# A hybrid recurrent and convolution block: other spacing of the heads' chains, 16x16 blocks copied on GpSimd, weight adds and one transpose placed by hand

## The chip, the cores and the metric

The kernel runs on one core of one Trainium2 chip. It is one launch with all inputs and the output in the chip's memory. The metric is the device time of one execution in microseconds (us). Engines are named as in the profile: PE is the matrix engine (PEld its weight loads), DVE the vector engine, ACT the scalar engine, POOL is GpSimd, and SP issues most of the loads and stores. Each engine works through its own instructions strictly in the order in which they were built into its queue; semaphores hold an instruction until its inputs are there and its output's buffer is free, and whatever stands behind it in the queue waits too.

## The reference

One layer for 512 tokens of width 1024, all in float32: a gated delta rule with 8 heads of 128, beside it a convolution branch, both gated and summed, then a SwiGLU feed-forward of width 2816 and a last norm.

```python
h = rmsnorm(x, norm1_w)
q, k, v, z, b_raw, a_raw, glu, gates = split(h @ w_in)
q, k, v = silu(causal_conv4(q, k, v));  q, k = l2norm(q), l2norm(k)
o = gated_delta_rule_chunked(q, k, v, g, beta)        # 8 heads
out_a = (rmsnorm(o, dn_norm_w) * silu(z)) @ dn_w_o
c = causal_conv31(ga * sigmoid(gb))
out_b = silu(layernorm(c)) @ cm_w_pw2 + cm_b_pw2
x = x + (gate_a * out_a + gate_b * out_b) @ w_out
h2 = rmsnorm(x, norm2_w)
x = x + (silu(f_gate) * f_up) @ ffn_w_down            # f_gate, f_up = split(h2 @ w_gate_up)
return rmsnorm(x, norm_f_w)
```

## The kernel before

Every large matmul is made as three passes of a shorter format. A weight block of 128x1024 is loaded as `raw`, ACT rounds it to `whi` (L107), DVE subtracts to get the rest, `wlo` (L108), and `split3` issues the passes (hh,whi), (hl,whi), (hh,wlo) at L117, where `hh` and `hl` are the rounded value and the rest of the activations. There are three buffers for such weight units. Outputs are tiles of 128 channels by 512 tokens, so most matmuls are 512 wide.

The program has these parts, with their times in the profile of before:

- 0 to about 85 us: input norm, transposes, the small projections, the first convolution inputs.
- about 85 to 350: the eight heads. `head` (L713) makes four projections of a head (k, q, v, z); `front` (L397) and `front2` (L451) make the head's small matrices for its four chunks of 128 tokens, and `chain` (L467) the four steps of the recurrence (L540 to L573). The heads' projections are interleaved with "other" projections (the convolution branch's `glu`, then gates), handed out by `take(8)`.
- to 483: the rest of the gates; then to about 533 the output projection `wo` of the heads (L812), among it the layer norm of the convolution branch: `ln_mean` (L629) at tile 2, `ln_norm` (L645) at tile 5.
- to 580 `wpw`, to 623 `wout` with the second norm and its transposes (L883 to L905), to 859 the feed-forward's first half, to 973 the down projection (`two`, L1119) and the last norm.

A `step` is about an eighth of a projection (three matmuls 512 wide); `count` numbers the steps. A chain for head n is begun once `count` has come to `START + ROUND * n` (84 + 40 n), and each of its pieces then says after how many steps the next one comes. Its pieces are put `behind()` the marked instructions of the large stream, which pins their place on each engine. Every 40 steps `background()` issues pieces of the 31-tap convolution (`conv31`, L612, 30 operations of DVE for each of eight channel blocks).

In `front` the inverse of a triangular 128x128 matrix is begun with 16x16 blocks: `Un` (L419 ACT, L420 POOL) is the matrix; four copies `cp` take its 32x32 diagonal blocks (L425, ACT), `cc` picks the two 16x16 blocks of each (L427 ACT, L428 DVE), `cc` is stored and loaded again in another layout as `U` (L430, L433, SP), and GpSimd solves the blocks in 30 small operations (L446, L448). `Ud` (L437, POOL) is the masked `Un`. `front2` makes `Vp` (L456, ACT, four pieces), read from a matmul result `g` of which there are two buffers; in the recurrence `w` (L552, ACT) takes a result of PE from `st`, and PE's next matmul of the chain (L555) needs `w`.

GpSimd also adds weights ahead of time. Sums of the down projection's blocks are made in halves: a load (`U`, later `wsh`, one buffer), four adds (`dsums_add`, L167) and a store (`wsum`, L168). The other stream is `s` (L191): DMAs with an add, issued from GpSimd's queue. In the layer norm, GpSimd sums the squares in seven adds (L642, tile `sacc`), and PE's matmul at L647 reads that sum.

At the end of `wout`, PE transposes the third block of tokens (`transposes(2)`), starts the first three tiles of the feed-forward on the first 256 tokens (`k_loop` over `first`, 256 wide), then transposes the fourth block (`transposes(3)`); ACT and DVE make `hh` (L904) and `hl` (L905) of each.

Of the kernel before, what the change touches and what calls it, by code (L numbers as in the profile page):

```python
# [6 lines left out]
F32 = mybir.dt.float32  # L7
# [16 lines left out]
PAD3 = 368  # L24
START = 84
ROUND = 40
EPS = 1e-6


@with_exitstack  # L30
def block_kernel(ctx, tc, a):
# [131 lines left out]

    def dsums_add(k, r, cs=slice(0, T)):
        b11, b12, b21, b22 = (r[:, i, :] for i in range(4))
        for o, x, y in ((b22, b12, b22), (b12, b11, b12), (b11, b22, b11), (b21, b11, b21)):
            G.tensor_tensor(out=o, in0=x, in1=y, op=ALU.add)  # L167
        nc.gpsimd.dma_start(wsum[k][:, :, cs], r)  # L168

    def half_load():  # L170
# [214 lines left out]

    def decay(h):

        DT = gp.tile([P, NT, P], F32, name="DT", bufs=2)
        nc.sync.dma_start(DT.rearrange("p n t -> p (n t)"),
                          mrow[h].rearrange("n t -> (n t)").partition_broadcast(P))  # L390
        G.tensor_tensor(out=DT, in0=DT, in1=neg.rearrange("p (a t) -> p a t", a=1).broadcast_to([P, NT, P]),
                        op=ALU.add)
        for n in range(NT):
            S.activation(DT[:, n, :], DT[:, n, :], AF.Exp, bias=nmc[:, n, h:h + 1])
        return DT

    def front(h, kT, DT):  # L397
        sq = junk[:, 0:P]

        ss = gp.tile([P, 8, NT], F32, name="ss", bufs=5)  # L400
        ps = tok(kT, psg, "g")
        for n in range(NT):
            S.activation(sq, ps[:, n, :], AF.Square, accum_out=ss[:, 0, n:n + 1])
        kd = gp.tile([P, 3, P], F32, name="kd", bufs=3)
        for n in range(3):
            S.activation(kd[:, n, :], ps[:, n, :], AF.Copy, scale=kdf[:, n, h:h + 1])
        kk, rk, nk, nb2, b2 = ss[:, 3], ss[:, 4], ss[:, 5], ss[:, 6], ss[:, 7]
        V.tensor_scalar(out=kk, in0=ss[:, 0], scalar1=EPS, scalar2=None, op0=ALU.add)
        V.reciprocal(out=rk, in_=kk)
        G.tensor_tensor(out=nk, in0=kk, in1=root4, op=ALU.pow)  # L410
        V.tensor_tensor(out=nb2, in0=rk, in1=nbeta[:, :, h], op=ALU.mult)
        V.tensor_tensor(out=b2, in0=rk, in1=beta[:, :, h], op=ALU.mult)

        ps = psg.tile([P, 4, P], F32, name="g")
        for n in range(NT):
            PE.matmul(ps[:, n, :], kT[:, n, :], kT[:, n, :], start=True, stop=True)
        Un = gp.tile([P, NT, P], F32, name="Un", bufs=3)
        for n in range(NT):
            S.activation(Un[:, n, :], ps[:, n, :], AF.Copy, scale=nb2[:, n:n + 1])  # L419
        G.tensor_tensor(out=Un, in0=Un, in1=DT, op=ALU.mult)  # L420

        cp = gp.tile([P, NT, 32], F32, name="cp")
        for b in range(4):
            b32 = slice(32 * b, 32 * b + 32)
            S.copy(out=cp[b32], in_=Un[b32, :, b32])  # L425
        cc = gp.tile([P, NT, 16], F32, name="cc")
        S.activation(cc, cp[:, :, 0:16], AF.Copy, scale=mh1)  # L427
        V.scalar_tensor_tensor(out=cc, in0=cp[:, :, 16:32], scalar=mh2, in1=cc, op0=ALU.mult, op1=ALU.add)  # L428
        sc = dram.tile([8, 16, NT, 16], F32, name="sc")
        nc.sync.dma_start(sc.rearrange("b k n c -> (b k) n c"), cc)  # L430
        U = gp.tile([P, 16, NT, 16], F32, name="U", bufs=2)
        for b in range(8):
            nc.sync.dma_start(U[16 * b:16 * b + 16].rearrange("p k n c -> p (k n c)"),  # L433
                              sc[b].rearrange("k n c -> (k n c)").partition_broadcast(16))

        Ud = gp.tile([P, NT, P], F32, name="Ud", bufs=3)
        G.tensor_tensor(out=Ud, in0=Un, in1=mc.rearrange("p (a t) -> p a t", a=1).broadcast_to([P, NT, P]),  # L437
                        op=ALU.mult)


        y = gp.tile([P, NT, 16], F32, name="y", bufs=3)
        S.copy(out=y, in_=idc.rearrange("p (a c) -> p a c", a=1).broadcast_to([P, NT, 16]))
        for k in range(15):
            w = 15 - k
            tm = gp.tile([P, NT, 16], F32, name="ytm")
            G.tensor_tensor(out=tm[:, :, 0:w], in0=U[:, k, :, k + 1:],  # L446
                            in1=y[:, :, k:k + 1].broadcast_to([P, NT, w]), op=ALU.mult)
            last[0] = G.tensor_tensor(out=y[:, :, k + 1:], in0=y[:, :, k + 1:], in1=tm[:, :, 0:w], op=ALU.add)  # L448
        return ss, kd, b2, Un, Ud, y
# [207 lines left out]
    def step():  # L657

        while queue:
            try:  # L660
                next(queue[0])
            except StopIteration:
                queue.pop(0)
                continue
            count[0] += 1
            if count[0] % ROUND == 0:
                background()
            return True
        return False
# [85 lines left out]
    rest = others()  # L755
    for h in range(H):
        queue.append(head(h, done))
        queue.append(take(8))
    queue.append(rest)
    nh = 0  # L760
    while step() or chains:
        start_feed[0] = count[0] >= 335
        if nh < H and count[0] >= START + ROUND * nh:
            chains.append([0, chain(*done[nh])])
            nh += 1
        for c in list(chains):
            if c[0] <= count[0] or not queue:
                with behind():
                    n = next(c[1], None)
                if n is None:  # L770
                    chains.remove(c)
                else:
                    c[0] = count[0] + n
# [104 lines left out]
    def norm2(hf, n, cs):  # L878
        rms_half(ss2, hf, n, cs, tp.tile([P, T], F32, name="sg"), hf)
        if hf:  # L880
# [4 lines left out]
            if n == NT - 1:  # L885

                transposes(2)
                for f in (0, FF, 1):
                    first.append((psw.tile([P, T], F32, name="w"), unit(a["wgu"][f])))
                for ps, w in first:  # L890
                    k_loop(ps, w, slice(0, 2 * P))
                transposes(3)

    def transposes(n):

        ts = slice(n * P, (n + 1) * P)
        for j in range(2):
            ps = psm.tile([P, 4, P], F32, name="mm")
            with behind(mybir.EngineType.PE):
                for c in range(4):  # L900
                    k = 4 * j + c
                    PE.transpose(ps[:, c, :], xs2[:, n, k * P:(k + 1) * P], ident)
            k4 = slice(4 * j, 4 * j + 4)
            S.activation(hh[:, k4, ts], ps, AF.Copy)  # L904
            V.tensor_tensor(out=hl[:, k4, ts], in0=ps, in1=hh[:, k4, ts].bitcast(F32), op=ALU.subtract)  # L905

    first = []

# [210 lines left out]
    def two(weights, xs, banks, then, also=(), k0=0):  # L1119
# [3 lines left out]
        for k in range(FK):  # L1123
# [3 lines left out]
                    nc.sync.dma_start(*also.pop(0))  # L1127
            for i in range(2):
                prods(w, i, xs[k], i, banks[2 * i:2 * i + 2], k == 0, k == FK - 1)
            if left:  # L1130
                with behind():
                    left.pop(0)()
            if k > 1:
# [153 lines left out]
```

## Time and profile before

| | |
|---|---|
| median of three runs | 975.8 us (973.53 to 977.41) |
| the profiled execution | 975.02 us |
| its span, first to last instruction | 973.2 us |
| PE busy | 942.7 us, 97% |
| DVE busy | 730.4 us, 75% |
| ACT busy | 537.9 us, 55% |
| POOL busy | 347.9 us, 36% |
| granted clock of PE, mean | 0.995 of full speed |

PE is the engine to follow: it is busy for nearly the whole span, so the time can only fall where PE stands still or is slow, and only grows where PE is made to wait. In a timeline row the first number is the start, the second the length; in brackets stands how long the engine was idle before and which instruction ended that. A matmul 512 wide has a length of some 0.39 us but the next one starts 0.227 us after it, since they are pipelined; distances between starts are what counts.

### The profile page before, as it was taken

To read this page: it belongs to the slowest core of one execution; us is meant where nothing else is said; L and a number is where in the kernel's file an instruction comes from. 1 tells how busy PE (TensorE), PEld (TensorE's weight loads), DVE (VectorE), ACT (ScalarE), POOL (GpSimd) and SP (SyncE) were. 2 spreads that over 40 slices of the span, in tenths; PEclk is the share of its full clock that TensorE was granted. 3 is DMA by queue.
4 is the path that set the end of the run, shared out by engine and by line. 5 is a ranking of instruction groups with operands and counts; after the bars stand their busy time and mean duration, and the time that the engine had idled before them with its cause. 6 is when DMAs were issued, how large, how long until landed. Compare 5 with 4: busy or idle time off the path is not lost. (4 is left out here: it accounts for less than half of the span.)

```text
span 973.2 us, 14887 instructions
## 1 busy us (share of the span) xinstructions
PE 942.7 (97%) x5199; PEld 795.3 (82%) x5199; DVE 730.4 (75%) x1125; ACT 537.9 (55%) x1130; POOL 347.9 (36%) x516
## 2 busy tenths in 40 slices
PE   7999999999999999999998999999999999999996
PEld 5687878878787888888886888888889999988875
DVE  4898988878888868889667753666434787789775
ACT  6688768678767573543536332333323554556544
POOL 0314524424252345254253442254441111134225
PEclk9999999999999999999999999999999999999998
DMA  8233422313222247688987985488899656577654
GB/s 316 86 128 100 142 78 66 99 44 122 81 84 89 76 132 217 180 258 286 299 253 233 272 254 162 174 242 281 282 266 222 205 174 196 171 225 246 225 180 143
DMA packets 78300, 177.40 MB, mean 182 GB/s; under 512 B 10209, under 2 KB 19329, under 8 KB 77201
## 3 DMA queue, kind: packets, MB, share of 16 engines
q1 hardware_dynamic: 66816, 144.88, 44.7%
q0 software_dynamic: 10256, 28.89, 12.9%
q10 hardware_dynamic: 1152, 2.69, 0.7%
q8 instruction: 41, 0.67, 0.3%
q14 instruction: 35, 0.28, 0.1%
HBM read 156.22 MB, written 45.37 MB: 207 GB/s over the span
## 5 line engine op out<-in xcount | busy, mean ns | idle before, releaser
L107 ACT ACTIVATE whi<-raw 128x1024 fp32r<-128x1024 f32 (+1 forms) x191 | 196.2, 1029 | 253.4 <-PE mm L117 154.3
L108 DVE TENSOR_TENSOR wlo<-raw,whi 128x1024 fp32r<-128x1024 f32 (+1 forms) x191 | 239.6, 1255 | 93.8 <-ACT whi L107 92.7
L117 PE MATMUL mm<-hh,whi 128*128 128x512 f32 (+1 forms) x688 | 269.5, 392 | 0.0
L117 PE MATMUL mm<-hl,whi 128*128 128x512 f32 (+1 forms) x688 | 263.5, 383 | 2.3 <-POOL hl L298 1.7
L117 PE MATMUL mm<-hh,wlo 128*128 128x512 f32 (+1 forms) x688 | 264.7, 385 | 0.5 <-DVE wlo L108 0.5
L612 DVE SCALAR_TENSOR_TENSOR cps<-c,c31w,cps 128x512 f32<-128x512 f32 x240 | 180.0, 750 | 5.7 <-ACT cps L610 1.6
L117 PEld LDWEIGHTS mm<-hl,whi 128*128 128x128 f32 x688 | 129.9, 189 | 24.7 <-POOL hl L298 2.9
L117 PEld LDWEIGHTS mm<-hh,wlo 128*128 128x128 f32 x688 | 129.6, 188 | 24.3 <-DVE wlo L108 0.9
L117 PEld LDWEIGHTS mm<-hh,whi 128*128 128x128 f32 x688 | 129.8, 189 | 21.0 <-ACT hh L297 0.2
L939 POOL TENSOR_TENSOR fm<-fm 128x256 f32<-128x256 f32 x33 | 30.1, 914 | 113.7 <-DVE s L939 91.9
L446 POOL TENSOR_TENSOR ytm<-U,y 128x60 f32<-128x60 f32 (+14 forms) x120 | 37.4, 311 | 53.3 <-DMA U<-sc 39.0
L370 DVE SCALAR_TENSOR_TENSOR acc<-mm,c4w,acc 128x511 f32<-128x511 f32 (+2 forms) x72 | 53.0, 738 | 2.1 <-ACT acc L367 1.7
L117 PE MATMUL mm<-yh,whi 128*128 128x512 f32 x128 | 51.3, 401 | 0.0
L117 PE MATMUL mm<-yh,wlo 128*128 128x512 f32 x128 | 50.5, 395 | 0.0
L117 PE MATMUL mm<-yl,whi 128*128 128x512 f32 x128 | 50.3, 393 | 0.0
L117 PE MATMUL w<-hl,whi 128*128 128x256 f32 x168 | 47.5, 283 | 1.1 <-DVE hl L905 1.1
L117 PE MATMUL w<-hh,wlo 128*128 128x256 f32 x168 | 47.6, 284 | 0.8 <-DVE wlo L108 0.8
L117 PE MATMUL w<-hh,whi 128*128 128x256 f32 x168 | 47.3, 284 | 0.2 <-ACT hh L904 0.2
L117 PE MATMUL w<-wlo,fh 128*128 128x512 f32 (+1 forms) x115 | 44.5, 387 | 0.6 <-DVE wlo L108 0.6
L117 PE MATMUL w<-whi,fl 128*128 128x512 f32 (+1 forms) x115 | 44.2, 385 | 0.0
L117 PE MATMUL w<-whi,fh 128*128 128x512 f32 (+1 forms) x115 | 44.2, 384 | 0.0
L191 POOL DMA_DIRECT2D s<-in_wgu_dram x24 | 22.6, 957 | 54.4 <-DMA s<-in_wgu_dram 54.4
(320 smaller groups left out, 1912.5 us busy)
## 6 DMA issues: line engine op xcount, KB each, us to landing
raw<-in_win_dram SPq DMA_DIRECT2D x61, 512.0 KB, 3.5
raw<-in_wgu_dram SPq DMA_DIRECT2D x32, 512.0 KB, 3.6
s<-in_wgu_dram SPq DMA_DIRECT2D x48, 256.0 KB, 5.7
raw<-s SPq DMA_DIRECT2D x48, 256.0 KB, 3.5
raw<-wsum SPq DMA_DIRECT2D x44, 256.0 KB, 4.2
raw<-in_wdn_dram SPq DMA_DIRECT2D x33, 256.0 KB, 4.1
s<-in_wgu_dram POOLq DMA_DIRECT2D x24, 256.0 KB, 6.6
s<-s POOLq DMA_DIRECT2D x24, 256.0 KB, 6.6
```

The source lines that it names most:

```text
L107: marked(S.activation(hi, raw, AF.Copy), "unit")
L108: marked(V.tensor_tensor(out=lo, in0=raw, in1=hi.bitcast(F32), op=ALU.subtract), "unit")
L117: marked(PE.matmul(ps, l, r, start=first and i == 0, stop=last and i == 2))
L191: fed.append(nc.gpsimd.dma_start(*begun.pop(0), accum_op=ALU.add, max_dma_last_dim=2048))
L370: marked(V.scalar_tensor_tensor(out=acc[:, s:], in0=ps[:, :T - s], scalar=c4w[:, j, k:k + 1], in1=acc[:, s:], op0=ALU.mult, op1=ALU.add))
L446: G.tensor_tensor(out=tm[:, :, 0:w], in0=U[:, k, :, k + 1:], in1=y[:, :, k:k + 1].broadcast_to([P, NT, w]), op=ALU.mult)
L612: V.scalar_tensor_tensor(out=acc, in0=c[:, k:k + T], scalar=c31w[:, i, k:k + 1], in1=acc, op0=ALU.mult, op1=ALU.add)
L939: return eng.tensor_tensor(out=out, in0=in0, in1=in1, op=op)
```

## The change

1. `OTHERS` gives the first four heads 12 steps of other projections instead of 8, and a chain begins at `START + 32 * n + sum(OTHERS[:n])`, so at the same distance behind its head's projections.
2. `background()` is called every 8 steps instead of every 40.
3. From the second head on (`h` > 0) the copies `cp` and the two steps of `cc` move from ACT and DVE to GpSimd, as four copies, two multiplications and one add; `Ud` is pinned behind them; `DT` has three buffers.
4. The four adds of a weight sum are pinned behind GpSimd's last marked instruction (`last[0]`), which in the layer norm is the last add of squares.
5. The third `k_loop` is pinned behind `transposes(3)`, and `hl` is marked, so that what is placed later stands behind it.
6. In the down projection the leftover pieces (`left`) are taken only at every second `k`.

```diff
+OTHERS = (12, 12, 12, 12, 8, 8, 8, 8)
...
     def dsums_add(k, r, cs=slice(0, T)):
         b11, b12, b21, b22 = (r[:, i, :] for i in range(4))
-        for o, x, y in ((b22, b12, b22), (b12, b11, b12), (b11, b22, b11), (b21, b11, b21)):
-            G.tensor_tensor(out=o, in0=x, in1=y, op=ALU.add)
+        with tc.issue_after(last[0].ins):
+            for o, x, y in ((b22, b12, b22), (b12, b11, b12), (b11, b22, b11), (b21, b11, b21)):
+                G.tensor_tensor(out=o, in0=x, in1=y, op=ALU.add)
         nc.gpsimd.dma_start(wsum[k][:, :, cs], r)
...
-        DT = gp.tile([P, NT, P], F32, name="DT", bufs=2)
+        DT = gp.tile([P, NT, P], F32, name="DT", bufs=3)
...
         cp = gp.tile([P, NT, 32], F32, name="cp")
+        cc = gp.tile([P, NT, 16], F32, name="cc")
         for b in range(4):
             b32 = slice(32 * b, 32 * b + 32)
-            S.copy(out=cp[b32], in_=Un[b32, :, b32])
-        cc = gp.tile([P, NT, 16], F32, name="cc")
-        S.activation(cc, cp[:, :, 0:16], AF.Copy, scale=mh1)
-        V.scalar_tensor_tensor(out=cc, in0=cp[:, :, 16:32], scalar=mh2, in1=cc, op0=ALU.mult, op1=ALU.add)
+            (G.tensor_copy if h else S.copy)(out=cp[b32], in_=Un[b32, :, b32])
+        if h:
+            G.tensor_scalar(out=cc, in0=cp[:, :, 0:16], scalar1=mh1, scalar2=None, op0=ALU.mult)
+            G.tensor_scalar(out=cp[:, :, 0:16], in0=cp[:, :, 16:32], scalar1=mh2, scalar2=None, op0=ALU.mult)
+            c_ = G.tensor_tensor(out=cc, in0=cc, in1=cp[:, :, 0:16], op=ALU.add)
+        else:
+            S.activation(cc, cp[:, :, 0:16], AF.Copy, scale=mh1)
+            V.scalar_tensor_tensor(out=cc, in0=cp[:, :, 16:32], scalar=mh2, in1=cc, op0=ALU.mult, op1=ALU.add)
...
-        G.tensor_tensor(out=Ud, in0=Un, in1=mc.rearrange("p (a t) -> p a t", a=1).broadcast_to([P, NT, P]),
-                        op=ALU.mult)
+        with tc.issue_after(c_.ins) if h else nullcontext():
+            G.tensor_tensor(out=Ud, in0=Un, in1=mc.rearrange("p (a t) -> p a t", a=1).broadcast_to([P, NT, P]),
+                            op=ALU.mult)
...
-            if count[0] % ROUND == 0:
+            if count[0] % 8 == 0:
                 background()
...
-        queue.append(take(8))
+        queue.append(take(OTHERS[h]))
...
-        if nh < H and count[0] >= START + ROUND * nh:
+        if nh < H and count[0] >= START + 32 * nh + sum(OTHERS[:nh]):
             chains.append([0, chain(*done[nh])])
...
-                for ps, w in first:
+                for ps, w in first[:2]:
                     k_loop(ps, w, slice(0, 2 * P))
-                transposes(3)
+                with tc.issue_after(transposes(3).ins):
+                    k_loop(*first[2], slice(0, 2 * P))
...
-            V.tensor_tensor(out=hl[:, k4, ts], in0=ps, in1=hh[:, k4, ts].bitcast(F32), op=ALU.subtract)
+            marked(V.tensor_tensor(out=hl[:, k4, ts], in0=ps, in1=hh[:, k4, ts].bitcast(F32), op=ALU.subtract), "hl")
+        return t
...
-            if left:
+            if left and k % 2:
                 with behind():
                     left.pop(0)()
```

How the orders of the engines move is shown at three places. The lines of code are numbered eight or more higher after the change.

The first is ACT in the third head. Before, the copies `cp` and `cc` stand among the large stream's work, `w` directly behind the copies and `Vp` further on:

```order
L419 ACTIVATE Un<-g,ss 128x128 x4
L373 ACTIVATE vT<-acc_1503 128x512
L570 ACTIVATE pa,ss<-o 128x128
L425 COPY cp<-Un 32x128 x4
L552 ACTIVATE w<-st,ss 128x128
L427 ACTIVATE cc<-cp,cst 128x64
L731 ACTIVATE A<-mm 128x512
L456 ACTIVATE Vp<-g,ss 128x128 x4
```

After:

```order
L421 ACTIVATE Un<-g,ss 128x128 x4
L375 ACTIVATE vT<-acc_1552 128x512
L576 ACTIVATE R<-st,sm 128x128
L739 ACTIVATE A<-mm 128x512
L481 ACTIVATE yb<-y,cst 128x4x16
L482 ACTIVATE yb<-y,cst 128x4x16
L108 ACTIVATE whi<-raw 128x1024
L578 ACTIVATE pa,ss<-o 128x128
L486 COPY Ye<-yb 32x4x32 x2
L560 ACTIVATE w<-st,ss 128x128
L464 ACTIVATE Vp<-g,ss 128x128 x4
```

The copies are gone from this queue, and the four `Vp` pieces now stand directly behind a `w`.

The second is GpSimd at the layer norm inside `wo`. Before, a set of weight adds stands ahead of the seven adds of squares:

```order
L191 DMA s_124<-in_wgu_dram 128x512
L167 TENSOR_TENSOR wsh<-wsh 128x256 x4
L168 DMA wsum<-wsh 512x1x256
L191 DMA s_127<-s_125 128x512
L642 TENSOR_TENSOR sacc<-sacc,acc_5220 128x512
```

After (the six further adds of squares, which differ in the number of `acc` alone, stand between the third and the fourth row):

```order
L193 DMA s_124<-in_wgu_dram 128x512
L193 DMA s_127<-s_125 128x512
L650 TENSOR_TENSOR sacc<-sacc,acc_5227 128x512
L169 TENSOR_TENSOR wsh<-wsh 128x256 x4
L170 DMA wsum<-wsh 512x1x256
```

The four weight adds and their store have changed places with the seven adds of squares; the DMA with an add (`s`) is still ahead of them.

The third is DVE at the first tiles of the feed-forward. Before:

```order
L905 TENSOR_TENSOR hl<-mm,hh 128x4x128 x2
L108 TENSOR_TENSOR wlo<-raw,whi 128x1024
L883 SCALAR_TENSOR_TENSOR xs_5890<-A,ss_5889,nw_5525 128x512 x2
L108 TENSOR_TENSOR wlo<-raw,whi 128x1024
L939 TENSOR_TENSOR xb_6372<-hh,hl 128x1024
L905 TENSOR_TENSOR hl<-mm,hh 128x4x128 x2
```

After:

```order
L914 TENSOR_TENSOR hl<-mm,hh 128x4x128 x2
L109 TENSOR_TENSOR wlo<-raw,whi 128x1024
L891 SCALAR_TENSOR_TENSOR xs_5897<-A,ss_5896,nw_5532 128x512 x2
L109 TENSOR_TENSOR wlo<-raw,whi 128x1024
L914 TENSOR_TENSOR hl<-mm,hh 128x4x128 x2
L949 TENSOR_TENSOR xb_6379<-hh,hl 128x1024
```

The sum `xb` and the last `hl` have changed places. On PE, the eight transposes of the fourth block stand ahead of the 24 matmuls of the third `k_loop` instead of behind them.

More of the change, by code (lines that the diff above doesn't have):

```diff
@@ L901, in transposes @@
                     k = 4 * j + c
-                    PE.transpose(ps[:, c, :], xs2[:, n, k * P:(k + 1) * P], ident)
+                    t = PE.transpose(ps[:, c, :], xs2[:, n, k * P:(k + 1) * P], ident)
             k4 = slice(4 * j, 4 * j + 4)
             S.activation(hh[:, k4, ts], ps, AF.Copy)
-            V.tensor_tensor(out=hl[:, k4, ts], in0=ps, in1=hh[:, k4, ts].bitcast(F32), op=ALU.subtract)
+            marked(V.tensor_tensor(out=hl[:, k4, ts], in0=ps, in1=hh[:, k4, ts].bitcast(F32), op=ALU.subtract), "hl")
+        return t
     first = []
```

## The prediction

> **What bounds the kernel now.** I began with the page's first part, which shows how long each engine is busy:
>
> ```profile
> span 973.2 us, 14887 instructions
> PE 942.7 (97%) x5199; PEld 795.3 (82%) x5199; DVE 730.4 (75%) x1125; ACT 537.9 (55%) x1130; POOL 347.9 (36%) x516
> ```
>
> PE stands still for only 973.2 - 942.7 = 30.5 us in all. The change leaves the matmuls as they are, so what it can win is a part of these 30.5 us, and time in which PE runs at a lower clock. The next view is the windows, busy time by stretch (columns: sum, busy time of PE, PEld, DVE, ACT and POOL with counts, clock, DMA share, GB/s):
>
> ```profile
> 100.00:150.00 50.00, 48.62 (x281) 40.06 (x280) 44.43 (x77) 37.09 (x107) 21.40 (x47) 1.00 0.37 118
> 200.00:250.00 50.00, 48.90 (x306) 39.63 (x305) 38.28 (x80) 41.19 (x115) 16.29 (x36) 1.00 0.26 80
> 475.00:500.00 25.00, 25.00 (x110) 20.35 (x109) 12.37 (x14) 8.75 (x12) 5.50 (x6) 1.00 1.03 356
> 500.00:525.00 25.00, 21.52 (x87) 17.00 (x86) 18.97 (x15) 9.85 (x13) 19.62 (x17) 0.93 0.67 215
> 625.00:650.00 25.00, 23.20 (x171) 21.67 (x169) 16.71 (x17) 6.34 (x10) 11.32 (x9) 1.00 0.86 253
> ```
>
> The holes are in the layer norm (500 to 525: PE misses 3.5 us and its clock falls to 0.93), at the first feed-forward tiles (625 to 650: 1.8 us), and thinly in the heads (1.1 to 1.4 us in 50). The waits of PE name them (us in total, times, longest):
>
> ```profile
> PE g L263 <- DVE cv L245: 7.1, 1, 7.1
> PE mm L647 <- POOL sacc L642: 3.5, 1, 3.5
> PE st L555 <- ACT w L552: 3.2, 4, 1.1
> PE w L117 <- DVE hl L905: 1.1, 1, 1.1
> PE g L383 <- ACT Vp L456: 1.0, 1, 1.0
> PE st L550 <- DVE R L547: 1.0, 1, 1.0
> PE w L117 <- DVE wlo L108: 1.4, 3, 0.6
> ```
>
> The 7.1 us at L263 lie before the heads and aren't touched. The others lie where the change works.
>
> **Part A, the heads: -2.2 us.** Four waits for `w` cost 3.2 us. One of them, in the timelines of ACT and PE:
>
> ```profile
> 136.44 1.22 ACT L425 COPY cp<-Un 32x128 f32<-32x128 f32 x4 [0.61 <-POOL Un L420]
> 137.68 0.37 ACT L552 ACTIVATE w<-st,ss 128x128 f32<-128x128 f32 x1
> 138.10 0.49 PE L555 MATMUL st<-w,kd 128*128 128x128 f32 x2 [1.09 <-ACT w L552]
> ```
>
> ACT came to the copies 0.61 us before `Un` was there, then copied for 1.22 us, and only then made the `w` on which PE stood for 1.09 us. In the new order no copy stands on ACT from the second head on, so this cause is gone: with `w`, `Vp` and `R`, for which PE waits on ACT's or DVE's lateness in the same way, it is 3.2 + 1.0 + 1.0 = 5.2 us. What is late next is `Vp`. Its four pieces now stand directly behind `w`; the matmul result they read is one of two buffers `g`, and PE's next `g` must wait until they have read it. The trace has one such wait, 1.0 us. I bound the new waits by none and by 1.0 in each of six heads, and take 0.5: 3.0 us stay, so A = 3.0 - 5.2 = **-2.2**, with ends -5.2 and +0.8.
>
> The copies on GpSimd aren't in the trace. The nearest rows by size:
>
> ```profile
> L446 POOL TENSOR_TENSOR ytm<-U,y 128x60 f32<-128x60 f32 x8 | 2.9, 359 | 44.6 <-DMA U<-sc 39.0 <-DMA raw<-in_win_dram 5.6
> L437 POOL TENSOR_TENSOR Ud<-Un,cst 128x512 f32<-128x512 f32 x8 | 11.1, 1387 | 0.6
> L298 POOL TENSOR_TENSOR hl<-xt,hh 128x512 fp32r<-128x512 f32 x4 | 7.6, 1919 | 12.8 <-ACT hh L297 12.8
> ```
>
> A copy has 128 elements in a partition, so it costs between 0.36 us (60 elements) and 1.92 (512, the slowest row); I take 0.5, near the small row. The three steps of `cc` have 64 elements, 0.36 each. A head then adds 4 x 0.5 + 3 x 0.36 = 3.1 us to GpSimd, with ends 2.5 and 8.8. Its solve waits 39.0 us in six heads for its data, so there is room; `sc`, `U` and the solve come a little later, and no row of PE's waits names the solve. I count nothing for it. The third buffer of `DT`, and `background` every 8 steps, cost nothing on PE: in the changed order 109 of the 240 operations of L612 stand ahead of the thirtieth weight unit where 100 did, so DVE's load moves little.
>
> More steps among the first heads put the last chain nearer to `wo`. In the timeline of before (PE, then DVE) the last transposes of a head, the split it feeds, and `wo`:
>
> ```profile
> 466.53 0.60 PE L383 MATMUL b<-cst,o 128*128 128x128 f32 x4
> 470.16 4.90 DVE L800 TENSOR_TENSOR yl<-A,yh 128x512 fp32r<-128x512 f32 x8 [1.11 <-ACT yh L799]
> 483.31 0.39 PE L117 MATMUL mm<-yh,whi 128*128 128x512 f32 x1
> ```
>
> There are 72 matmuls between the first and the last of these rows; now there are 24, 24 x 0.227 = 5.4 us. The last head's block is the eighth of the split, and `wo` takes a block every 3 x 0.227 = 0.68 us while the split makes one in 4.90 / 8 = 0.61, so PE needs only the first blocks at once, which come from older heads. Counted at 0; the other end is 3 us, if the whole split were to wait behind that head.
>
> **Part B, the layer norm's sums: -4.8 us.** GpSimd, then PE:
>
> ```profile
> 496.77 4.35 POOL L167 TENSOR_TENSOR wsh<-wsh 128x256 f32<-128x256 f32 x4 [0.33 <-DMA wsh<-in_wdn_dram]
> 502.11 1.00 POOL L191 DMA_DIRECT2D s<-s  x1
> 502.68 12.32 POOL L642 TENSOR_TENSOR sacc<-sacc,acc 128x512 f32<-128x512 f32 x7
> 515.05 1.12 PE L647 MATMUL mm<-sacc,cst 128*128 128x512 f32 x2 [3.48 <-POOL sacc L642]
> 516.47 0.62 PE L117 MATMUL mm<-yh,wlo 128*128 128x512 f32 x1
> 519.88 0.40 PE L117 MATMUL mm<-yl,whi 128*128 128x512 f32 x1
> ```
>
> PE came to L647 at 515.05 - 3.48 = 511.57 and stood until the seventh add. Behind that, from 516.47 to 519.88, eight matmuls take 3.41 us where they take 8 x 0.227 = 1.82 at full clock: 1.6 us more. Together 5.1 us. In the new order the four weight adds stand behind the seven adds of squares, which then wait only for the DMA with an add ahead of them. Its input is the load that SP issued, by SP's timeline and the list of DMA issues in this stretch (median to landing), at 491.45 + 7.8 = 499.25:
>
> ```profile
> 491.45 0.50 SPq L187 DMA_DIRECT2D s<-in_wgu_dram  x1
> s<-in_wgu_dram SPq DMA_DIRECT2D x2, 256.0 KB, 7.8
> ```
>
> The adds began 502.68 - 502.11 = 0.57 us behind that DMA, so now at 499.8. Seven of them take between 7 x 1.39 = 9.7 us (`Ud`'s row, the same size) and 12.32 as before: they end between 509.5 and 512.1, and PE comes at 511.57. I take a wait of 0.3 on average, and the half clock gone: B = 0.3 - 5.1 = **-4.8**; the ends are -5.1, and -1.1 if the DMA comes as late as before (rival 2). The weight adds now end some 12 us later, and the next `wsh` load waits for them on SP with weight loads behind it; three weight buffers stand between that and PE, so nothing is counted.
>
> What the Trainium skill says of the clock ("TensorE: Matmul & The Clock Gate", section "What's actually happening") is that half rate is the state after an idle window of about 3.4 us, and that the window runs freely. The trace agrees: 3.48 us of waiting were followed by half clock, and none of the waits of 1.1 us and less were, as the clock of 1.00 in their windows shows. By that rule a wait of 0.3 leaves the clock alone, and B is as above; a wait near 3 could still cost the 1.6.
>
> **Part C, the fourth transpose: -2.0 us.** PE, then DVE:
>
> ```profile
> 630.88 0.39 PE L117 MATMUL w<-hh,wlo 128*128 128x256 f32 x1 [0.45 <-DVE wlo L108]
> 633.61 1.04 PE L902 MATMUL mm<-cst,xs 128*128 128x128 f32 x8
> 634.89 0.62 PE L117 MATMUL w<-hh,whi 128*128 128x256 f32 x3 [0.25 <-ACT hh L904]
> 636.62 0.39 PE L117 MATMUL w<-hl,whi 128*128 128x256 f32 x1 [1.10 <-DVE hl L905]
> 629.60 1.22 DVE L108 TENSOR_TENSOR wlo<-raw,whi 128x1024 fp32r<-128x1024 f32 x1
> 634.74 1.22 DVE L939 TENSOR_TENSOR xb<-hh,hl 128x1024 f32<-128x1024 f32 x1 [3.92 <-DMA s<-in_wgu_dram]
> 635.88 1.28 DVE L905 TENSOR_TENSOR hl<-mm,hh 128x512 fp32r<-128x512 f32 x2
> ```
>
> PE waits 0.45 + 0.25 + 1.10 = 1.8 us here: for the third tile's `wlo`; for `hh` of the block just transposed; for its `hl`, which DVE made only after `xb` (1.22 us). The transposes (1.04 us) now come ahead of the third tile, so they fill the wait for its `wlo`, and its 24 matmuls lie between the transposes and the first use of the block. `hl` stands ahead of `xb`. Start to start each of these gaps is some 0.15 us longer than the idle time given, 2.2 in all. All three should go; I take **-2.0**, with ends -2.2 and -0.9 (if `xs`, which DVE finishes just before the `wlo` at 629.60, is late and the transposes wait instead).
>
> **Part D, the down projection: -0.4 us.** One more wait for `wlo`, 0.6 us, the longest in its row, comes at 930.9. DVE, then GpSimd:
>
> ```profile
> 928.52 2.31 DVE L108 TENSOR_TENSOR wlo<-raw,whi 128x1024 fp32r<-128x1024 f32 x1
> 928.34 3.64 POOL L939 TENSOR_TENSOR y<-y,v 128x512 f32<-128x512 f32 x2 [0.96 <-DVE v L939]
> ```
>
> The `wlo` took 2.31 us beside GpSimd's adds, where the one above took 1.22. With pieces at every second `k` the adds meet fewer weight units. I take -0.4, between -0.8 and +0.4 (an add may meet another).
>
> **Sum.** -2.2 - 4.8 - 2.0 - 0.4 = -9.4 against the profiled execution's 975.0 us (span 973.2 and 1.8 around it), which is 0.8 below the median of the runs, 975.8. So **965.6 us**. A measurement tells about 0.5% from no change, 4.9 us: faster means below 970.9, slower above 980.7.
>
> **Rivals.**
>
> 1. The heads' waits only move. In every later head PE waits 1.0 for `Vp` and A comes to +0.8: 968.6. For it: `Vp` is directly behind `w` in the new order; against: one such wait is in the trace, not six. Chance 0.22.
> 2. GpSimd comes to the sums as late as before. For it: the DMAs are full just before (share 1.03 in 475 to 500), and loads that now come later in SP's order, the input `x` among them, meet there; the DMA with an add, which stands ahead of the sums, may start 2.5 us later. The sums then end near 514, the wait is some 2.4 and the clock may still halve: B = -1.1, the time 969.3. Against: that load's own place hardly moves. Chance 0.15. With rival 1 on top it is 972.3, within 0.5%; so is any case in which two parts fail: 0.12.
> 3. Slower: DVE becomes the bound in heads 2 to 4. DVE is busy 44.43 of 50 us there; a head lasts (350 - 85) / 8 = 33 us, so DVE has 33 x 5.57 / 50 = 3.7 us of its own, less 9 x 0.75 / 4 = 1.7 for the convolution operations that come earlier. A GpSimd operation and one of DVE with two inputs slow each other (2.31 against 1.22). If every microsecond added on GpSimd were lost to DVE, PE would wait from 2.0 us a head on; at the high end, 8.8, 6.8 us in each of the three: 965.6 + 20.4 = 986. It is slower than 980.7 from (15.1 / 3 + 2.0) = 7.0 us a head on, that is from (7.0 - 1.1) / 4 = 1.5 us a copy. Against: 1.5 is the price of 512 elements, and a copy has 128; DVE's most frequent operation there, L612, reads one large operand. Chance 0.04.
> 4. The change doesn't do what it says: the gaps go, but PE, early by 2 us, meets loads that are full from 475 to 500, and gives A back at `wo`: 967.8. Chance 0.07.
>
> The Trainium skill ("SBUF — State Buffer", section "SBUF: two separate sides") has the port that DVE and GpSimd share as an exclusive lock, held for a whole instruction, against operations of DVE with two inputs. The trace agrees as far as 2.31 against 1.22 goes; by that rule rival 3's loss is one to one only for such operations.
>
> **How the numbers follow.** The forecast has 0.40. All good ends together give 975.0 - 5.2 - 5.1 - 2.2 - 0.8 = 961.7, and the range begins there; it reaches over rivals 1, 2 and 4 and the cases with two failures to 972.5. Faster by over 0.5%: 0.40 + 0.22 + 0.15 + 0.07 = 0.84, less 0.02 for the part of rival 2 that lies above 970.9: 0.82. Within 0.5%: 0.12 + 0.02 = 0.14. Slower: 0.04.
>
> **What would show it.** A: the row of waits for `w` falls from 3.2 below 1, and one for `Vp` comes up to some 3. B: `sacc` begins near 500 in the old time, no clock below 1.00 about 500 to 525, and a wait at L647 below 1. C: no wait for `hl` between 625 and 650, PE busy for 24.5 or more of 25. D: no wait for `wlo` behind 900. It is wrong if the copies take 1.5 us and `wlo` stretches in the heads, if `wo` begins with a wait for the split, or if the clock is below 1.00 in a new place.

## The result, and the profile after

The changed kernel takes 964.17 us (median of five runs, 962.76 to 967.98) against 975.8 us, a ratio of 0.9887 with a 95% interval of 0.986 to 0.9914. In a later comparison on one chip the same kernel gave 0.9884 (0.9868 to 0.99). The forecast was 965.6 us, with a range from 961.7 to 972.5.

The profiled execution took 964.17 us, with a span of 961.9. Lines of code stand one to ten numbers higher than before: L107 is L108 now, L905 is L914. The page's first part after the change:

```profile
span 961.9 us, 14869 instructions
PE 941.8 (98%) x5199; PEld 793.8 (83%) x5199; DVE 731.8 (76%) x1118; ACT 529.4 (55%) x1095; POOL 357.4 (37%) x565
```

PE's work is the same (941.8 against 942.7 us), so the 11.3 us come out of the time in which it stood still or ran slowly. The windows after, in the columns of before:

```profile
100.00:150.00 50.00, 50.00 (x287) 40.96 (x286) 43.42 (x77) 36.60 (x104) 27.29 (x61) 1.00 0.31 97
500.00:525.00 25.00, 25.00 (x110) 20.20 (x108) 18.95 (x20) 17.50 (x24) 16.43 (x15) 1.00 0.62 192
625.00:650.00 25.00, 25.00 (x151) 22.40 (x150) 17.64 (x13) 6.76 (x8) 12.87 (x12) 1.00 0.92 270
```

All three holes are closed, and the clock is 1.00 in the layer norm. The waits of PE, where the lines left out lie ahead of the heads or are 0.3 us and less:

```profile
PE g L265 <- DVE cv L247: 7.2, 1, 7.2
...
PE mm L118 <- DVE yl L808: 0.6, 1, 0.6
...
PE w L118 <- DVE wlo L109: 0.5, 2, 0.3
PE b L514 <- DVE Xd L502: 0.5, 1, 0.5
...
PE st L563 <- ACT w L560: 0.3, 1, 0.3
```

The 5.2 us for `w`, `Vp` and `R` have become 0.3, the 3.5 at the sum of squares is gone, and a wait for `yl` is new. It lies in the second split, which makes the high and low part of the layer norm's result for `wpw`. Where the time went can be read by setting the starts of the same PE instructions side by side (us from the span's start):

| PE instruction | before | after | change since the row above |
|---|---|---|---|
| first matmul of a large projection | 36.11 | 37.08 | +1.0 |
| first matmul of `wo` | 483.31 | 479.62 | -4.7 |
| 20 matmuls behind the variance sum | 522.16 | 513.20 | -5.3 |
| last matmul of `wpw` | 577.24 | 569.46 | +1.2 |
| first matmul of the down projection | 858.91 | 848.27 | -2.9 |
| last matmul | 964.84 | 953.59 | -0.6 |

The first row isn't the change's: that place lay between 34.8 and 37.1 in the profiles of this study, of whatever kernel. What differs there is mostly how long PE's first matmuls, from 7 us on, stand 0.43 us apart instead of 0.227: to 11.3 us in the profile of before, to 13.2 in this one. Below, times up to `wo` are therefore counted from this first row.

### The profile page after: what moved, and what is told of

Its sections match the earlier page's. It is cut to its first block, busy times and chain, and to the rows that moved or that the text cites. A ratio compares the mean times of both kernels' runs of the same rounds, so it can differ in the third digit from the quotient of the medians.

```text
span 961.9 us, 14869 instructions
## 1 busy us (share of the span) xinstructions
PE 941.8 (98%) x5199; PEld 793.8 (83%) x5199; DVE 731.8 (76%) x1118; ACT 529.4 (55%) x1095; POOL 357.4 (37%) x565
## 4 chain that ended last, share of the span: by engine, by line
PE 90%; DVE 4%; ACT 2%; POOL 2%; issue 1%; DMA 1%; SPq 0%; POOLq 0%; ACTq 0%; DVEq 0%
PE mm L118 59%; PE w L118 20%; PE g L385 1%; PE st L564 1%; PE g L418 1%; PE st L558 1%; DVE wlo L109 1%; PE b L490 1%; PE st L563 1%; PE b L496 1%; DMA gsl<-sgd 1%; POOL ss L879 1%; PE b L514 1%; PE st L552 1%; PE g L467 1%
## 5 line engine op out<-in xcount | busy, mean ns | idle before, releaser
L108 ACT ACTIVATE whi<-raw 128x1024 fp32r<-128x1024 f32 (+1 forms) x191 | 196.4, 1030 | 246.8 <-PE mm L118 151.1
L109 DVE TENSOR_TENSOR wlo<-raw,whi 128x1024 fp32r<-128x1024 f32 (+1 forms) x191 | 242.3, 1270 | 95.9 <-ACT whi L108 95.3
L454 POOL TENSOR_TENSOR ytm<-U,y 128x60 f32<-128x60 f32 (+14 forms) x120 | 31.8, 265 | 48.6 <-DMA U<-sc 30.9
L456 POOL TENSOR_TENSOR y<-y,ytm 128x60 f32<-128x60 f32 (+14 forms) x120 | 39.0, 325 | 9.4
```

The lines of the kernel that those rows point to most:

```text
L108: marked(S.activation(hi, raw, AF.Copy), "unit")
L109: marked(V.tensor_tensor(out=lo, in0=raw, in1=hi.bitcast(F32), op=ALU.subtract), "unit")
L454: G.tensor_tensor(out=tm[:, :, 0:w], in0=U[:, k, :, k + 1:], in1=y[:, :, k:k + 1].broadcast_to([P, NT, w]), op=ALU.mult)
```

## The experiments

Each run was timed beside the kernel before on the same chip; ratios are to that kernel, with the 95% interval in brackets.

### Parts taken away from the changed kernel

**The copies back on ACT.**

```diff
-            (G.tensor_copy if h else S.copy)(out=cp[b32], in_=Un[b32, :, b32])
-        if h:
+            S.copy(out=cp[b32], in_=Un[b32, :, b32])
+        if False:
...
-        with tc.issue_after(c_.ins) if h else nullcontext():
+        with nullcontext():
```

> The changed kernel with the copies cp and both steps of cc back on ACT and DVE; all else stays. Theory 1 (the copies in ACT's queue were what made w, Vp and the like late): the heads lose most of the 4.7 us that they won, waits of PE for w, Vp or R come back to 3 to 5 us in all, time 967 to 969. Rival (the wider spacing of the first four chains gave PE work to go on with, and the copies did not matter): the waits in the heads stay below 2 us and the time within 1 us of the changed kernel, 964 to 965.

Measured: 969.73 us, 0.9958 (0.9944 to 0.9972), from 967.3 to 972.3 in ten executions. The waits of this run in the heads:

```profile
PE st L563 <- ACT w L560: 1.9, 4, 1.2
PE st L558 <- DVE R L555: 1.5, 2, 0.8
```

`w` and `R` are late again, and from the first large projection to `wo` the profile takes 447.9 us against 442.5 in the changed kernel, 5.4 more: the whole gain of the heads is gone. Theory 1 held, with a time just above its range. The prices of the moved instructions on GpSimd, in the groups of the changed kernel:

```profile
L428 POOL COPY cp<-Un 32x128 f32<-32x128 f32 x28 | 9.8, 350 | 1.3
L430 POOL TENSOR_SCALAR cc<-cp,cst 128x64 f32<-128x64 f32 x7 | 3.2, 452 | 0.7
L431 POOL TENSOR_SCALAR cp<-cp,cst 128x64 f32<-128x64 f32 x7 | 4.2, 601 | 0.7
L432 POOL TENSOR_TENSOR cc<-cc,cp 128x64 f32<-128x64 f32 x7 | 3.0, 433 | 0.6
```

That is (9.8 + 3.2 + 4.2 + 3.0) / 7 = 2.9 us a head, and one `wlo` takes 1270 ns in the mean of the changed kernel, against 1255 before.

**Eight steps behind each head again.**

```diff
-OTHERS = (12, 12, 12, 12, 8, 8, 8, 8)
+OTHERS = (8,) * 8
```

> The changed kernel with 8 steps of other projections behind each head again. Theory 1 (copies): the waits in the heads stay below 2.5 us, time within 1 us of the changed kernel's 964.2. Rival (spacing): PE's waits in the heads rise by 3 us or more, in the first four heads, and the time is 967 or more.

Measured: 978.34 us, 1.0047 (1.0032 to 1.0063): slower even than the kernel before, which neither theory expected. But the waits didn't rise in the heads: PE comes to `wo` after 441.4 us, 1.2 earlier than in the changed kernel. The largest of them, with DVE's timeline at its end:

```profile
PE mm L639 <- DVE sacc L626: 9.7, 1, 9.7
```

```profile
490.82 6.29 DVE L620 SCALAR_TENSOR_TENSOR cps<-c,c31w,cps 128x512 f32<-128x512 f32 x8
497.78 0.69 DVE L626 TENSOR_TENSOR sacc<-sacc,cv 128x512 f32<-128x512 f32 x1 [0.67 <-ACT cv L622]
```

The 31-tap convolution is still running on DVE when PE needs the sum over its channels, which opens the layer norm. Its last operation is at 496 us, where it was at 476 in the kernel before and is at 452 in the changed one. Behind this wait the clock is low too (0.94 between 500 and 525). None of this was in the forecast, so the next run took it apart.

**Eight steps, and two buffers of `DT`.** In DVE's order, the last convolution operation of the run above stands behind the 78th weight unit; with two `DT` buffers, and nothing else altered, it stands behind the 74th, as in the kernel before.

```diff
-OTHERS = (12, 12, 12, 12, 8, 8, 8, 8)
+OTHERS = (8,) * 8
...
-        DT = gp.tile([P, NT, P], F32, name="DT", bufs=3)
+        DT = gp.tile([P, NT, P], F32, name="DT", bufs=2)
```

> The changed kernel with 8 steps behind each head and with two DT buffers again. It tells apart why 8 steps with the rest of the change gave 978. Theory (with the third buffer DVE's order takes up the convolution more slowly at that spacing: its last operation stands behind the 78th weight unit, with two buffers behind the 74th as before): the wait of 9.7 us at the layer norm's mean goes, the convolution ends near 476, and the time is 10 us or more below that run, 964 to 969. Rival (the wider spacing is what keeps the convolution on time): PE still waits over 5 us for DVE's sacc and the time stays above 973.

Measured: 967.26 us, 0.9917 (0.9899 to 0.9936), 11 us below the run with three buffers. The last convolution operation is at 476 us and the wait at the mean is gone. So it was the third buffer that made the convolution late at that spacing, and with the wider spacing it doesn't; why the order on DVE moves so is not shown. With two buffers, on the other hand, a wait of 2.3 us for `Q` near 112 us is there, with a low clock behind it (0.95 and 0.71 in the two windows from 110 to 120), and `wo` is reached after 445.7 us, 4.3 later than with three. Against the changed kernel on the same chip this run is 0.9917 - 0.9884 = 0.3%, some 3 us, slower, about the width of the intervals; that is the worth of the wider spacing and the third buffer together; the rest of the change with 12 steps and two buffers was not run.

**The weight adds ahead of the squares again.**

```diff
-        with tc.issue_after(last[0].ins):
+        with nullcontext():
             for o, x, y in ((b22, b12, b22), (b12, b11, b12), (b11, b22, b11), (b21, b11, b21)):
```

> The changed kernel with the four weight adds no longer pinned behind the adds of squares. Theory: they stand ahead of the squares again, PE waits 3.5 to 5 us for the sum, the clock falls below 1.00 behind it for 1.6 us, while the wait for yl (1.2 us with what follows it) goes, since SP's load of the next weight set no longer has to wait: time 968 to 970. Rival (GpSimd's place there did not matter, since the sum would have been awaited from DVE's differences anyway): no wait over 1 us, time 964 to 965.

Measured: 965.21 us, 0.9901 (0.988 to 0.9922), not to be told from the changed kernel. GpSimd's timeline and PE's wait:

```profile
490.01 4.38 POOL L169 TENSOR_TENSOR wsh<-wsh 128x256 f32<-128x256 f32 x4 [0.29 <-DMA wsh<-in_wdn_dram]
...
495.94 13.02 POOL L650 TENSOR_TENSOR sacc<-sacc,acc 128x512 f32<-128x512 f32 x7
```

```profile
PE mm L655 <- POOL sacc L650: 1.5, 1, 1.5
```

The adds are ahead of the squares as they were, yet PE waits only 1.5 us, and the clock stays at full rate. The weight load came earlier: the adds begin 0.1 us before the mean's matmul (at 490.11), while in the kernel before they began 2.6 us after it (496.77 against 494.19). And the wait for `yl` is gone. From the start of `wo` to behind the variance sum this profile takes 1.7 us more than the changed kernel's (35.3 against 33.6), from there to the end of `wpw` 1.2 less: the pin wins 1.7 us and gives back 1.2. The theory's place was right, its size was not: it had 968 to 970 us, and a low clock.

**The third tile ahead of the transposes again.**

```diff
-                for ps, w in first[:2]:
+                for ps, w in first:
                     k_loop(ps, w, slice(0, 2 * P))
-                with tc.issue_after(transposes(3).ins):
-                    k_loop(*first[2], slice(0, 2 * P))
+                transposes(3)
```

with `hl` not marked.

> The changed kernel with the third k_loop ahead of the fourth block's transposes again and hl unmarked. Theory: the three waits (for wlo, hh and hl, 0.45 + 0.25 + 1.10 us idle, 2.3 from start to start) come back, time 966 to 967. Rival: PE's waits there come back, but are taken up by waits that go later in the feed-forward, and the time stays within 0.7 us of 964.2.

Measured: 965.57 us, 0.9909 (0.9893 to 0.9925). The three waits are back (0.43, 0.25 and 1.10 us idle), and the down projection begins 2.4 us later than in the changed kernel, counted against the row ahead. The theory held in the trace; in the times alone the intervals overlap.

Putting the pace of `background()` back from 8 to 40 moves no instruction in any engine's queue of the built program, so part 2 of the change does nothing here. Part 6 was not tried alone, and neither was the third buffer of `DT` at the wider spacing.

### Parts put into the kernel before

**The copies alone**, as in part 3 of the change but with two `DT` buffers.

> The kernel before with the copies cp and both steps of cc on GpSimd from the second head on, Ud behind them; all else as before. Theory 1 (the copies are what PE waited for in the heads): the 5.2 us of waits for w, Vp and R fall below 1.5, the convolution keeps its place on DVE, so the layer norm's first sum is not awaited, and the time is 4 to 5 us below the kernel before. Rival (moving the copies pays only with the wider spacing; on its own it makes the convolution late, as in the run with 8 steps behind each head): PE waits some us for DVE's sacc at the layer norm's mean, and the time is the kernel before's within 2 us, or above it.

Measured: 973.38 us, 0.9998 (0.9984 to 1.0012): nothing. (Its profile comes to `wo` 1.4 us earlier, 445.8 against 447.2, which the times of ten executions don't show.) The waits for `w` and `R` did fall, from 4.2 to 1.1 us, and the one for `Vp` went, but there is a new one, and in the window behind it the clock is low:

```profile
PE b L494 <- ACT Q L490: 2.3, 1, 2.3
```

```profile
115.00:120.00 5.00, 5.00 (x19) 4.01 (x18) 4.89 (x12) 2.43 (x5) 3.81 (x11) 0.80 0.49 170
```

So the first theory is right on the cause and its rival on the outcome, though not by the convolution: the old waits went with the copies, and another took their place. It can be followed back on ACT and SP:

```profile
110.26 1.28 ACT L394 ACT_TABLE_LOAD   x1 [3.58 <-DMA DT<-mrow]
111.93 0.20 ACT L490 ACTIVATE Q<-b 128x64 f32<-128x64 f32 x1
```

```profile
105.27 0.33 SPq L435 DMA_DIRECT2D sc<-cc  x1
105.68 0.38 SPq L389 DMA_DIRECT2D DT<-mrow  x1
```

`Q` stands on ACT behind work on the next head's `DT`, and ACT waits 3.58 us for the load of `DT`. That load stands on SP behind the store of `cc` now, which GpSimd has ready at 105.24; in the kernel before it was issued at 102.23, ahead of the store at 104.03. With 12 steps the load of `DT` is behind the store as well (107.58 and 107.16 in the run with copies and spacing), but there ACT makes `Q` at 107.07, ahead of its work on `DT` from 113.48 on, and PE doesn't wait.

**The spacing alone**, as in part 1.

> The kernel before with 12 steps behind the first four heads and the chains begun accordingly; all else as before. Theory (the later chains put three of the four loads of x behind the load of the weight set, which lands earlier, so GpSimd's adds of squares begin earlier): the wait at the variance sum falls from 3.5 to about 1.5 us and the half clock behind it goes, 3.6 us less, while waits for w in the heads stay near 3 us. Rival (spacing acts in the heads): the waits in the heads fall below 2 us and the layer norm's wait stays at 3.5 with its half clock.

Measured: 973.73 us, 0.998 (0.9961 to 0.9999). At the variance sum the theory held: the wait is 1.7 us instead of 3.5, without half clock, 3.3 us less. In SP's order only one of the four loads of `x` stands ahead of the weight load, where all four did, and GpSimd's weight adds begin 0.1 us after the mean's matmul instead of 2.6. That the loads of `x` are the reason is read from this order; no run moves them alone. But up to `wo` the profile has lost 4.6 us (451.8 against 447.2), mostly to a new wait of 1.28 us and a stretch of half clock behind it. PE's timeline:

```profile
108.81 1.03 PE L483 MATMUL b<-xc,Ud 128*128 128x16 f32 x8 [1.28 <-DVE xc L476]
109.69 0.48 PE L118 MATMUL mm<-hh,whi 128*128 128x512 f32 x1
110.01 0.51 PE L118 MATMUL mm<-hl,whi 128*128 128x512 f32 x1
110.31 0.63 PE L118 MATMUL mm<-hh,wlo 128*128 128x512 f32 x1
110.74 0.63 PE L118 MATMUL mm<-hh,whi 128*128 128x512 f32 x1
...
116.72 0.52 PE L118 MATMUL mm<-hl,whi 128*128 128x512 f32 x1
```

From 110.3 to 116.7 the matmuls 512 wide stand 0.43 us apart instead of 0.227, which by these figures costs about half of 6.4 us, 3.2. The ten timed executions fall in two groups by mean clock: 971.1 us in the mean of the four at 0.998 and above, 975.0 in the six at 0.995 and below.

**Copies and spacing together.**

> The kernel before with both the copies on GpSimd and the 12 steps behind the first four heads, and none of the other parts. Theory (the two need each other: alone the copies gave a ratio of 0.9998 and the spacing 0.998, each with a new stretch of half clock near 112 us): the waits in the heads fall to 2 us, no half clock there or behind the variance sum, where the wait is 1.5 us, and the time is 7 to 9 us below the kernel before, ratio about 0.992. Rival (the parts add up): 1 to 2 us below, ratio 0.998.

Measured: 967.75 us, 0.9927 (0.9909 to 0.9945). Alone the two gave 0.02% and 0.2%, together 0.73%: they need each other, as the theory had it, since the spacing puts `Q` ahead of the late `DT`. PE reaches `wo` 4.2 us earlier than in the kernel before, counted from the first large projection (443.0 against 447.2), no window between 100 and 120 or 500 and 525 is below a clock of 1.00, and the variance sum is awaited for 1.7 us.

**The pin alone**, as in part 4.

> The kernel before with the four weight adds pinned behind the adds of squares; all else as before. Theory (they are what is ahead of the squares): the adds of squares begin some 2.5 us earlier, the wait of 3.5 falls to about 1 us and the half clock goes, 4 us less; the next load of a weight set then holds SP until the store has landed and 1.2 us are given back at the second split, so 2 to 4 us below the kernel before. Rival (the DMA with an add ahead of the squares is as late as before): the wait stays above 3 us and nothing is won.

Measured: 971.15 us, 0.9962 (0.9946 to 0.9977). Its waits at the two places:

```profile
PE mm L117 <- DVE yl L801: 1.4, 1, 1.4
...
PE mm L648 <- POOL sacc L643: 1.3, 1, 1.3
```

The sum is awaited 2.2 us less and the half clock (1.6 us) is gone; 2.0 us are given back at the split. The theory held in both its terms, the second being larger than expected. The sums begin at 500.96, 7.2 us behind the mean's matmul instead of 8.5: the DMA with an add, at 500.41, holds them.

### A version meant to be faster

The wait for `yl` in the changed kernel, from right to left: PE, DVE, SP and GpSimd.

```profile
525.98 0.50 PE L118 MATMUL mm<-yl,whi 128*128 128x512 f32 x1 [0.61 <-DVE yl L808]
```

```profile
523.50 0.69 DVE L822 TENSOR_TENSOR ma<-mm,gsl 128x512 f32<-128x512 f32 x1 [3.69 <-DMA gsl<-sgd]
```

```profile
505.24 0.53 SPq L801 DMA_DIRECT2D gsl<-sgd  x1
515.20 0.60 SPq L163 DMA_DIRECT2D wsh<-in_wdn_dram  x1
...
518.82 0.46 SPq L801 DMA_DIRECT2D gsl<-sgd  x1
```

```profile
507.58 4.04 POOL L169 TENSOR_TENSOR wsh<-wsh 128x256 f32<-128x256 f32 x4
511.93 0.81 POOL L170 DMA_DIRECT2D wsum<-wsh  x1 [0.30 <-POOL wsh L169]
```

`wsh` has one buffer. The weight adds now come late, so their store is issued only at 511.93, and SP stands at the next load of that buffer until 515.20. Behind it in SP's queue is the gate tile `gsl`, DVE waits 3.69 us for it, and `yl` stands behind that on DVE. The next kernel holds the weight loads back from the variance sum until the second split, so that one half is added in the feed-forward instead.

```diff
-        if halves and gps_ and units[0] > 3 and not taken and not norming[0] and (units
+        if halves and gps_ and units[0] > 3 and not taken and not norming[0] and not held[0] and (units
...
             norming[0] = False
+            held[0] = True
...
     yh, yl = zip(*[split(cv[k]) for k in range(KD)])
+    held[0] = False
```

> The changed kernel with the loads of weight halves held back from the layer norm's variance until the second split is built, so that one half fewer is added during wo and one more in the feed-forward. Theory (the wait for yl of 0.6 us, 1.2 us with what follows, comes from SP standing at the load of the next weight set until the store of the last has landed, with the gate's load behind it): that wait goes and the time is 1.2 us below the changed kernel, about 963. Rival (the half that moves into the feed-forward costs as much there, on GpSimd and DVE): 964 or more, with new waits between 620 and 860 us.

Measured: 963.03 us, 0.9882 (0.9854 to 0.991). The wait for `yl` is gone, and the profile gains 1.2 us between the variance sum and the end of `wpw`, which shows the cause; but a wait of 0.75 us for `wlo` is new at 748. Both were run again, five rounds side by side:

> The changed kernel once more, beside the next one on the same chip: about 964, a ratio of 0.989 to the kernel before, with one wait of 0.6 us for yl and no half clock.

> The changed kernel without a weight half loaded in the layer norm, as in the run before (ratio 0.9882 with a wide interval). Theory: the wait for yl is gone, 1.2 us, and some of it is given back where the half is now added in the feed-forward (0.9 us of a wait for wlo at 748 in that run): 0 to 1.2 us below the changed kernel. Rival: it gives all back and is within 0.3 us of it.

Measured: 964.06 us, 0.9884 (0.9868 to 0.99) for the changed kernel, 964.24 us, 0.9885 (0.9868 to 0.9903) for this one. The rival held: between the variance sum and the end of `wpw` it gains 1.4 us, and from there to the start of the down projection its profile loses 3.5 us, with two waits of 0.8 us at 752 for `whi` and `wlo` and a new stretch of half clock behind them:

```profile
745.00:760.00 15.00, 13.46 (x98) 13.05 (x97) 9.79 (x15) 5.68 (x8) 2.33 (x3) 0.89 0.81 218
```

So it isn't a better kernel: the two can't be told apart in time, and none of this study is clearly faster than the changed one.

## Why the prediction was right, and where it was not

The sum was -9.4 us, the profile has -11.3. By its own steps:

**A, the heads (-2.2; measured -4.7).** The mechanism was right: the copies on ACT were what PE waited for, as their return shows. The term that was mis-sized is the 3.0 us of new waits for `Vp`, 0.5 in each of six heads: there were none. Of the -5.2 that this leaves, 0.5 is taken by a new wait for `Xd`. ACT in the third head after the change:

```profile
144.71 0.37 ACT L560 ACTIVATE w<-st,ss 128x128 f32<-128x128 f32 x1 [0.60 <-PE st L558]
144.97 1.13 ACT L464 ACTIVATE Vp<-g,ss 128x128 f32<-128x128 f32 x4
```

Now ACT waits for PE, not PE for ACT: `w` comes at once, and the four `Vp` pieces are through 1.4 us after `w` began. The price of the moved work was right in its sum, 2.9 us a head against 3.1, and not in its parts: the copies took 1.4 us, where 2.0 were counted, and the three steps of `cc` 1.5, where 1.1 were.

But the step put this gain down to the copies alone, and counted nothing for the spacing of the chains beyond the nearness of the last one to `wo`. The runs show that the copies alone win nothing here, the spacing alone 0.2%, and both 0.73%. The place that the step left out is one that it named: "`sc`, `U` and the solve come a little later", of which it wrote "I count nothing for it". The store to `sc` does come later, the load of the next `DT` behind it on SP too, and with 8 steps and two buffers that costs a wait of 2.3 us and a low clock. That the whole change pays nothing for it is due to the order of `Q` and `DT` on ACT, which the prediction did not look at: here it was lucky.

**The third buffer of `DT` ("cost nothing on PE").** This is true only beside the wider spacing. With 8 steps it costs 1.0047 against 0.9917, by a convolution that ends 20 us later on DVE. The step read the order of the changed kernel as a whole, where 9 of the 240 operations had moved, and did not ask which part kept it there.

**B, the sums (-4.8; measured -5.3, less 1.2 given back at the split).** The sum begins earlier and ends 0.1 us before PE is there:

```profile
494.75 12.87 POOL L650 TENSOR_TENSOR sacc<-sacc,acc 128x512 f32<-128x512 f32 x7 [0.20 <-ACT acc L649]
507.73 1.07 PE L655 MATMUL mm<-sacc,cst 128*128 128x512 f32 x2
```

The place and the size were right, the share of the pin was not. With the pin alone the sums began at 500.96, not at 499.8, and PE waited 1.33 us, not 0.3. In the changed kernel only 1.7 of the 5.3 us are the pin's; the other wait, and the half clock, had gone already with the later chains, which moved the loads of `x` behind the weight load. The prediction saw that shift of the loads, in its rival 2, but only as something that could make GpSimd later. The failed step is the last of this part: the next `wsh` load "waits for them on SP with weight loads behind it", so "nothing is counted". It looked at the weight loads, which had three buffers, and not at the gate's load in the same queue.

**C, the transpose (-2.0; measured -2.3 in the sum of the gaps, 2.4 when undone).** Right. DVE makes `hl` ahead of `xb` and is done with it at 624.98, while the third tile's 24 matmuls keep PE busy until some 626.1:

```profile
623.69 1.29 DVE L914 TENSOR_TENSOR hl<-mm,hh 128x512 fp32r<-128x512 f32 x2 [0.66 <-ACT hh L913]
624.89 1.22 DVE L949 TENSOR_TENSOR xb<-hh,hl 128x1024 f32<-128x1024 f32 x1
```

Another 0.4 us from start to start at 751, a wait for `wlo`, also went; it was not forecast.

**D, the down projection (-0.4; measured -0.6).** The wait of 0.6 us for `wlo` is gone, one of 0.2 is left. It wasn't tried alone.

**The rivals.** 1 (the heads' waits move to `Vp`) fell. So did 2 in the changed kernel, where the sums begin 4.2 us behind the mean's matmul and not 8.5; with the pin alone, at 7.2, it was half true. And so did 3: `wlo` takes 1.2% longer in the mean, and PE waits for nothing of DVE between 100 and 150. A slower result by DVE was near all the same, by another way: the run with 8 steps and three `DT` buffers. Rival 4 fell, since `wo` begins 4.7 us earlier and nothing is late there.

## What to carry to other kernels

Where a scheduler sets the order, the parts of a change do not add up: undo them one at a time from the changed kernel as well as adding them one at a time to the old one, and look at the orders of all engines for each, since a third buffer that seemed free moved the work of another engine by 20 us. When work on a tile with one buffer is put later, follow the load that refills that buffer: its queue stands until then, and everything behind it in that queue is late, not only what is large (here the gate's load behind `wsh`). The same holds for a store whose data come later: with the copies alone, the load of `DT` behind `sc` took back what the copies had won.

## What the runs showed of the hardware

The half clock doesn't follow from the length of a wait alone. It came behind waits of 3.48 us (the kernel before), 9.7 us (8 steps) and 2.3 us (the copies alone, and 8 steps with two `DT` buffers, at 112 us), behind one of 1.28 us that eight matmuls 16 wide followed (the spacing alone), and behind two of 0.8 us with 0.5 us of work between them (the weight loads held back, run again, at 752). It did not come behind waits of 1.3 to 1.7 us at the variance sum in four other profiles, nor behind one of 2.7 us in the run with 8 steps.

Nor does it follow the end of the wait closely. In five of these places the matmuls went half as fast only 1.2 to 1.8 us after PE had gone on, and for 3.4 us (516.5 to 519.9 in the kernel before, 113.6 to 117.1 with the copies alone, 754.2 to 757.6 at the two short waits) or twice that (110.0 to 116.9 with the spacing alone). At the start of the program, where PE begins at about 7 us, they were slow until 9.0 to 13.2 us, differently in each profile.

The page "TensorE: Matmul & The Clock Gate" of the Trainium skill, section "What's actually happening", has half rate after an idle window of some 3.4 us; the 2.3 and the 1.28 us differ from that, and here the measurement decides. That the window runs freely, as the page also says, would fit the varying begin and executions of one kernel that fall in two groups by their clock; what decides, the small matmuls or the place in such a window, these runs leave open.
